# Two of the delta rule's gate projections moved forward in a hybrid decoder layer's list of dense work

## The chip, the cores and the metric

The kernel is one program on one NeuronCore of a Trainium2 chip. The metric is the device time of one execution in microseconds; smaller is better. Five engines run their own instruction queues in order and meet through semaphores: TensorE (PE, matmuls and transposes), VectorE (DVE), ScalarE (ACT), GpSimd (POOL) and SyncE (SP, which here issues all the DMAs).

## The reference, cut to what matters

One layer of a hybrid decoder, for a prompt of 1024 tokens and 8 sequences of 4 sampled tokens (1056 columns in all, model width 1024). A normalised input goes through one input projection. Its columns feed three token mixers: a gated delta rule (4 heads of 128), an mLSTM (4 heads of 64) and a Mamba-2 SSD (4 heads of 64). Their outputs go through one output projection, and a ConvFFN follows.

```python
conv_out = silu(causal_dwconv(proj[..., :CONV_DIM]))       # q, k, v of the delta rule; x, B, C of the SSD
o_gdn, gdn_new = gdn_chunked(q, k, v, g, beta, state)
o_gdn = rms_norm(o_gdn, gdn_norm) * silu(gg)               # gg: the delta rule's gate, 4 heads x 128
h_ml = rms_norm(sigmoid(mo) * mlstm_chunked(...))          # mo: 2 tiles of 128
y_ssd = rms_norm((ssd_chunked(...) + D * x) * silu(sz))    # sz: 2 tiles of 128
mix = concatenate([o_gdn, h_ml, y_ssd])
out = mix @ w_out
```

The three recurrences run in chunks of tokens, each chunk after the one before it.

## The kernel before

Activations lie transposed: features on the 128 partitions, tokens along the row. A dense tile is one block of 128 output features for all 1056 tokens: three groups of 352 columns, each a sum over 8 blocks of the input, each product made of three fp32r matmuls (high part by high part, high by low, low by high). So a tile is 72 matmuls of 128x352 (`dense`, whose matmuls all carry line 208). The result of a group lies in one of two PSUM banks named `acc` and is scaled into SBUF by DVE (line 308).

Dense work before the output projection is in units and gates. A unit is three tiles: units 0 to 3 are the heads of the delta rule (k, q, v), 4 and 5 the SSD's groups (B, C, x), 6 and 7 the mLSTM's pairs of heads. The tiles of units 0 to 5 go through a causal convolution of width 4 and a silu, on DVE (lines 473 and 482) and ACT. A gate is one tile: `gg` 0 to 3 for the delta rule's heads, `mo` 0 and 1 for the mLSTM, `sz` 0 and 1 for the SSD. A `gg` gate takes per group a scaling, a tanh on ACT, and on DVE a product (line 431) and a product with the head's output (433); for columns whose head has not been put out yet a single product (429), with the second one done where the head's output comes (1043).

The order on PE is written out by hand and in full. A class `Weave` runs generators, each with a rank, and keeps a clock of its own (`now`), which every matmul moves on by its length. A generator yields how long the other engines are expected to need (`WAIT`) before its next step. At each turn the lowest rank that is ready goes next. The recurrences have ranks 0 to 2, the samples' streams 3 to 5, and the dense work has rank 9, so dense matmuls fill PE's queue between the steps of the recurrences, and only what is left of them can. The order of DVE, ACT, POOL and SP follows from a scheduler that goes by the program's order and priorities.

`fill` takes the dense work from the list `FILL`, each time the first entry that may go. A unit may go while fewer than two units are in work, unit 2 (whose tiles lie in the buffer `mix`) as soon as the small rows are there. The gates `gg` 0 to 3 and `mo` 0 may go once the small rows are there, `mo` 1, `sz` 0 and `sz` 1 once six of the delta rule's eight passes are done:

```python
def can(n):
    if type(n) is int:
        return (n == U_MIX and "rows" in have) or (n != U_MIX and len(live) < 2)
    return "rows" in have and MIX[n] < 5 or done["gdn"] >= 2 * (U_MIX - U_GDN + 1)
```

The phases follow each other: the delta rule (8 passes of four chunks: `gdn_starts`, `gdn_blocks`, `gdn_pres`, `gdn_scans`), then the SSD (`ssd_scans`, `ssd_posts`), then the mLSTM (`ml_pres`, `ml_scans`, `ml_posts`; 4 passes of four chunks). When the mLSTM's last normalisation is done and the list is empty, the streams of the samples and the output projection are added (`samples`, `split_mix`, `project_first`). The projection's matmuls are 128x264, one for each quarter of the tokens; their operands are `mix`, cast on ACT (line 1582) and subtracted on DVE (1583).

The last steps of an mLSTM pass are these. `kq` is transposed (line 1120 makes `kwm` of it). Each of the four chunks has matmuls with `kwm`, `E` and the state `Cb`; DVE brings `Cb` up to date with two operations (1146) that the next chunk needs, and finishes `hml` with three (1151 to 1153) behind one on ACT. The normalisation (`gated_norm`) multiplies by the gate (1059), squares on ACT, sums (1063), scales (1064), takes a power on POOL (1065), multiplies (1066), transposes on PE and writes to `mix` on ACT.

The order of the list before: 0, 2, 1, `mo` 0, 3, 4, `sz` 0, `mo` 1, 5, `sz` 1, 6, 7, `gg` 0 to 3. What really ran on PE, by the entries' rules: 0, 1, 2, `mo` 0, 3, 4, `sz` 0, `mo` 1, `sz` 1, 5, 6, 7, `gg` 0, `gg` 1, `gg` 2, `gg` 3. By the trace `mo` 0 begins at 199.9 us, unit 3 at 225.1, unit 4 at 298.9, `sz` 0 at 362.5, unit 5 at 418.4, unit 6 at 471.3, unit 7 at 525.7, `gg` 0 at 580.3, `gg` 1 at 602.4, `gg` 2 at 620.5 and `gg` 3 at 633.2.

Of the kernel before, what the change touches and what calls it, by code (L numbers as in the profile page):

```python
# [49 lines left out]
U_MIX = 2  # L50
GATES = [("gg", h) for h in range(4)] + [("mo", 0), ("mo", 1), ("sz", 0), ("sz", 1)]

FILL = [0, 2, 1, ("mo", 0), 3, 4, ("sz", 0), ("mo", 1), 5, ("sz", 1), 6, 7, ("gg", 0), ("gg", 1), ("gg", 2), ("gg", 3)]
TILE_ORDER = [(s, i) for _, _, ts in UNITS for s, i, _ in ts] + GATES


# [141 lines left out]
def kernel(ctx: ExitStack, tc: tile.TileContext, I, O):  # L198
# [174 lines left out]
    with ExitStack() as ph:  # L373
# [169 lines left out]
        def fill():  # L543

            todo = [n for n in FILL if n not in have]
            while todo:
# [1666 lines left out]
```

## Time and profile before

| | |
|---|---|
| median of three runs | 1553.21 us (1550.89 to 1555.63) |
| the profiled execution | 1549.13 us, of it the span of the profile 1547.3 us |
| PE busy | 1456.2 us, 94% of the span |
| DVE busy | 1019.2 us, 66% |
| ACT, POOL busy | 605.3 us, 604.0 us |
| mean granted PE clock | 0.977 of 2.4 GHz |

PE is the engine to watch: the time is PE's work plus the time in which PE waits or runs at its lower clock. In the chain that ended last, PE's dense matmuls are the only large entry. The stretch that the change touches is from about 200 us to 655 us; there DVE is the second busy engine.

### The profile page before, as it was taken

How to read it: one execution, taken by the hardware profiler on the slowest of the kernel's cores; microseconds unless marked ns; L12 is line 12 of the kernel's file. 1: busy time of each engine (PE TensorE's matmuls, PEld its weight loads, DVE VectorE, ACT ScalarE, POOL GpSimd, SP SyncE). 2: the span in 40 equal slices, each digit the busy share in tenths (PEclk: the TensorE clock that was granted, in tenths of full speed). 3: DMA queues.
4: the chain of work that ended last, by engine and by line, in shares of the span. 5: the costliest groups of instructions: out<-in, count | busy, mean ns of one | idle time of the engine just before them, and what ended most of it. 6: DMA issues, size and time to landing. Idle time of an engine off the chain costs nothing. (4 is left out here: it accounts for less than half of the span.)

```text
span 1547.3 us, 27515 instructions
## 1 busy us (share of the span) xinstructions
PE 1456.2 (94%) x10756; PEld 1410.7 (91%) x10756; DVE 1019.2 (66%) x2014; ACT 605.3 (39%) x1316; POOL 604.0 (39%) x671
## 2 busy tenths in 40 slices
PE   9888999989989989899798999999999999999997
PEld 8787998879989989889698999999999999999996
DVE  6889878697375457723678777666666685234447
ACT  7644544533433233524475433333333344112222
POOL 6234433342343463367430434443443341212234
PEclk9989999999999999999899999999999999999998
DMA  6011010110121042312630211222222236312304
GB/s 224 30 50 31 23 45 26 36 32 18 43 59 60 29 119 94 100 69 97 210 136 33 90 59 71 73 83 70 83 84 70 83 103 236 120 48 98 111 26 157
DMA packets 60362, 124.92 MB, mean 81 GB/s; under 512 B 15544, under 2 KB 21560, under 8 KB 59720
## 3 DMA queue, kind: packets, MB, share of 16 engines
q1 hardware_dynamic: 60232, 123.16, 23.9%
q8 instruction: 85, 1.39, 0.4%
q14 instruction: 45, 0.37, 0.1%
HBM read 97.40 MB, written 25.21 MB: 79 GB/s over the span
## 5 line engine op out<-in xcount | busy, mean ns | idle before, releaser
L208 PE MATMUL acc<-h,wh 128*128 128x264 f32 (+1 forms) x3040 | 677.2, 313 | 17.5 <-DVE pre L308 12.3
L208 PEld LDWEIGHTS acc<-h,wh 128*128 128x128 f32 x3040 | 496.6, 191 | 24.4 <-DVE pre L308 8.7
L208 PE MATMUL acc<-h,wl 128*128 128x264 f32 (+1 forms) x1528 | 466.2, 305 | 0.3 <-POOL wl L619 0.2
L208 PEld LDWEIGHTS acc<-h,wl 128*128 128x128 f32 x1528 | 290.5, 190 | 1.5 <-POOL wl L619 1.5
L208 PE MATMUL acc<-hidl,wh 128*128 128x264 f32 x576 | 163.7, 284 | 0.5 <-DVE hidl L2033 0.5
L208 PE MATMUL acc<-hidh,wh 128*128 128x264 f32 x576 | 163.9, 285 | 0.0
L208 PE MATMUL acc<-hidh,wl 128*128 128x264 f32 x576 | 163.5, 284 | 0.0
L1874 POOL TENSOR_TENSOR wl<-ws,wh 128x512 fp32r<-128x512 f32 x60 | 89.3, 1495 | 161.0 <-ACT wh L1873 156.4
L2056 DVE TENSOR_TENSOR fa<-fa,acc 128x264 f32<-128x264 f32 x160 | 68.2, 427 | 125.6 <-PE acc L208 125.1
L272 POOL TENSOR_TENSOR wl<-w,wh 128x1024 fp32r<-128x1024 f32 x42 | 104.1, 2479 | 70.3 <-ACT wh L271 67.5
L208 PE MATMUL acc<-n,wh 128*128 128x264 f32 x640 | 119.3, 284 | 0.6 <-DVE n L1948 0.6
L208 PEld LDWEIGHTS acc<-hidl,wh 128*128 128x128 f32 x576 | 108.6, 189 | 0.7 <-DVE hidl L2033 0.7
L208 PEld LDWEIGHTS acc<-hidh,wl 128*128 128x128 f32 x576 | 108.6, 189 | 0.0
L208 PEld LDWEIGHTS acc<-hidh,wh 128*128 128x128 f32 x576 | 108.5, 188 | 0.0
L2047 POOL TENSOR_TENSOR wl<-w,wh 128x1024 fp32r<-128x1024 f32 (+1 forms) x22 | 47.6, 2163 | 147.7 <-ACT wh L2046 144.8
L208 PEld LDWEIGHTS acc<-n,wh 128*128 128x128 f32 x640 | 98.7, 188 | 0.8 <-issue 0.8
L1874 POOL TENSOR_TENSOR wl<-w,wh 128x512 fp32r<-128x512 f32 x40 | 64.9, 1625 | 81.0 <-ACT wh L1873 75.3
L208 PE MATMUL acc<-n,wl 128*128 128x264 f32 x320 | 91.4, 286 | 2.7 <-POOL wl L1874 2.7
L208 PE MATMUL acc<-r,wh 128*128 128x264 f32 x480 | 90.5, 286 | 2.8 <-DVE rs L1850 2.8
L208 PEld LDWEIGHTS acc<-r,wh 128*128 128x128 f32 x480 | 73.9, 188 | 4.6 <-DVE rs L1850 4.6
L1806 DVE SCALAR_TENSOR_TENSOR fy<-fpre,vec,fy 128x1072 f32<-128x1072 f32 x44 | 75.1, 1730 | 3.2 <-ACT fy L217 2.7
L2046 ACT CAST wh<-w 128x1024 fp32r<-128x1024 f32 (+1 forms) x22 | 20.5, 933 | 132.4 <-PE acc L208 127.8
(533 smaller groups left out, 3034.0 us busy)
## 6 DMA issues: line engine op xcount, KB each, us to landing
w<-in_w_in_dram SPq DMA_DIRECT2D x30, 512.0 KB
w<-in_w_up_dram SPq DMA_DIRECT2D x60, 256.0 KB
hid_dram<-hid SPq DMA_DIRECT2D x22, 528.0 KB
hidl<-hid_dram SPq DMA_DIRECT2D x21, 528.0 KB
w<-in_w_dn_dram SPq DMA_DIRECT2D x17, 512.0 KB
w<-in_w_out_dram SPq DMA_DIRECT2D x16, 512.0 KB
E<-rows_dram SPq DMA_DIRECT2D x24, 256.0 KB
n<-in_w_up_dram SPq DMA_DIRECT2D x20, 256.0 KB
```

The lines of the kernel that those rows point to most:

```text
L208: return nc.tensor.matmul(out, **kw)
L272: tt(out=wl[:, ks], in0=w[:, ks], in1=wh[:, ks].bitcast(F32), op=ALU.subtract)
L1806: stt(out=y[:, :LF], in0=pre[:, j:j + LF], scalar=col(V_FW + 3 * f + j), in1=y[:, :LF], op0=ALU.mult, op1=ALU.add)
L1874: tt(out=wl, in0=x, in1=wh.bitcast(F32), op=ALU.subtract)
L2046: nc.scalar.copy(out=wh, in_=w)
L2047: gtt(out=wl, in0=w, in1=wh.bitcast(F32), op=ALU.subtract)
L2056: vtt(out=fa[:, q, m, :], in0=fa[:, q, m, :], in1=ps[:, :Q], op=ALU.add)
```

## The change

One list is changed: `gg` 0 comes behind unit 2 and `gg` 1 behind `mo` 0.

```diff
-FILL = [0, 2, 1, ("mo", 0), 3, 4, ("sz", 0), ("mo", 1), 5, ("sz", 1), 6, 7, ("gg", 0), ("gg", 1), ("gg", 2), ("gg", 3)]
+FILL = [0, 2, ("gg", 0), 1, ("mo", 0), ("gg", 1), 3, 4, ("sz", 0), ("mo", 1), 5, ("sz", 1), 6, 7, ("gg", 2), ("gg", 3)]
```

What runs on PE by the entries' rules is now 0, 1, 2, `gg` 0, `mo` 0, `gg` 1, 3, 4, `sz` 0, `mo` 1, `sz` 1, `gg` 2, 5, 6, 7, `gg` 3. Up to the end of unit 2 nothing changes. `gg` 2 moves too, though its place in the list does not: when `sz` 1 is done, two units are still in work, so unit 5 may not go and `gg` 2 is the first entry that may. Three gates, 216 dense matmuls, so leave the end of the mixing phase, and one stays. The steps of the recurrences keep their own order. The number of matmuls is the same.

While the delta rule's last pair of passes is prepared, PE's order has 30, 42, 21, 84, 21 and 51 dense matmuls in a row (unit 4 and the end of unit 3), with four or eight transposes or four products between them. Before, the same preparation lay under unit 4 together with a whole pass of the scan.

PE's queue, the last chunk of the mLSTM's last pass and the end of its normalisations. `mc<-Cb` is the product with the state, `gsq` the transposes of a normalisation, `acc<-h` 128x352 a dense matmul and 128x264 one of the projection. Before:

```order
L208 MATMUL mb<-va_5824,kwm 128x130
L208 MATMUL mc<-va_5824,E_6336 128x130 x2
L208 MATMUL mc<-Cb,kq 128x130
L208 MATMUL acc<-h_155,wh 128x352
L208 MATMUL acc<-h_163,wh 128x352
L208 MATMUL acc<-h_155,wl 128x352
L208 MATMUL acc<-h_156,wh 128x352
L208 MATMUL acc<-h_164,wh 128x352
L208 MATMUL acc<-h_156,wl 128x352
L212 MATMUL mb<-con,gsq 128x128 x4
```

Now, from the third chunk to the projection's first matmuls:

```order
L212 MATMUL mb<-con,mix 128x128 x4
L208 MATMUL mb<-va_6111,kwm 128x130
L208 MATMUL mc<-va_6111,E_6623 128x130 x2
L208 MATMUL mc<-Cb,kq 128x130
L208 MATMUL mb<-va_6111,kwm 128x130
L208 MATMUL mc<-va_6111,E_6623 128x130 x2
L208 MATMUL mc<-Cb,kq 128x130
L212 MATMUL mb<-con,gsq 128x128 x4
L212 MATMUL mb<-con,mix 128x128 x4
L212 MATMUL mb<-con,gsq 128x128 x4
L208 MATMUL acc<-h_6850,wh 128x264
L208 MATMUL acc<-h_6852,wh 128x264
```

Behind the transposes of `kq` in the last pass the order before had runs of 9, 6, 9, 9, 6, 21, 42 and 114 dense matmuls (216) before the projection; now it has none.

DVE's queue from `kwm` of the last pass on. Before:

```order
L1120 TENSOR_TENSOR kwm<-mb,wk__6354 128x512
L429 SCALAR_TENSOR_TENSOR mix<-pre 128x32
L431 SCALAR_TENSOR_TENSOR pre<-pre 128x320
L433 TENSOR_TENSOR mix<-mix,pre 128x320
L1146 SCALAR_TENSOR_TENSOR Cb<-Cb,wib,mb 64x65 x2
L1151 TENSOR_TENSOR dn<-dn,em 128x2
L1152 RECIPROCAL dn<-dn 128x2
L1153 TENSOR_TENSOR hml<-mc,dn 128x128
L1059 SCALAR_TENSOR_TENSOR hml<-mb,hml 128x512
L1146 SCALAR_TENSOR_TENSOR Cb<-Cb,wib,mb 64x65 x2
```

Now:

```order
L1120 TENSOR_TENSOR kwm<-mb,wk__6641 128x512
L1583 TENSOR_TENSOR h_6871<-mix,h_6869 128x1056
L1146 SCALAR_TENSOR_TENSOR Cb<-Cb,wib,mb 64x65 x2
L429 SCALAR_TENSOR_TENSOR mix<-pre 128x32
L1151 TENSOR_TENSOR dn<-dn,em 128x2
L431 SCALAR_TENSOR_TENSOR pre<-pre 128x320
L1146 SCALAR_TENSOR_TENSOR Cb<-Cb,wib,mb 64x65 x2
L1059 SCALAR_TENSOR_TENSOR hml<-mb,hml 128x512
L1151 TENSOR_TENSOR dn<-dn,em 128x2
L1152 RECIPROCAL dn<-dn 128x2
```

A subtraction for the projection's operand (line 1583) now stands between `kwm` and the first update of `Cb`, and a second one stands further down, ahead of the third update.

ACT's queue at the same place (`dn` is the operation in each chunk that line 1151 waits for; `h_6842` is the decay of the delta rule's samples, whose input comes by a DMA into a buffer of the dense work's operands; `h_6869` is the projection's operand). Before:

```order
L217 ACTIVATE dn<-mc 128x2 x2
L271 CAST wh<-w 128x1024
L217 ACTIVATE pre<-pre 128x352
L217 ACTIVATE dn<-mc 128x2
L217 ACTIVATE gsq<-hml 128x512
L217 ACTIVATE dn<-mc 128x2
L217 ACTIVATE pre<-pre 128x352
```

Now:

```order
L217 ACTIVATE h_6842<-h_6842 128x128
L217 ACTIVATE h_6842<-h_6842,sneg 128x128
L217 ACTIVATE dn<-mc 128x2
L271 CAST wh<-w 128x1024
L1582 CAST h_6869<-mix 128x1056
L217 ACTIVATE pre<-pre 128x352
L332 ACT_TABLE_LOAD
L217 ACTIVATE dn<-mc 128x2 x2
L217 ACTIVATE gsq<-hml 128x512
```

The samples' decay, a cast for the projection and a load of an activation table have moved in between the chunks.

## Rows read from the trace of the kernel before

**Rows 1.** The profile's page, busy time of each engine over the whole span.

```profile
PE 1456.2 (94%) x10756; PEld 1410.7 (91%) x10756; DVE 1019.2 (66%) x2014; ACT 605.3 (39%) x1316; POOL 604.0 (39%) x671
```

**Rows 2.** Busy time by stretch (us: PE, weight loads, DVE, ACT, POOL; clock; DMA).

```profile
200.00:299.00 99.00, 94.11 (x668) 89.48 (x667) 77.91 (x207) 46.92 (x156) 34.50 (x60) 0.98 0.11 33
299.00:363.00 64.00, 56.17 (x354) 52.60 (x353) 56.88 (x140) 24.92 (x82) 22.25 (x35) 0.95 0.10 28
363.00:418.00 55.00, 54.28 (x389) 52.48 (x388) 25.31 (x54) 19.93 (x61) 14.51 (x21) 1.00 0.13 42
418.00:526.00 108.00, 100.53 (x662) 98.00 (x661) 64.16 (x148) 38.15 (x79) 49.20 (x58) 0.97 0.16 49
526.00:602.00 76.00, 71.01 (x472) 68.52 (x471) 41.12 (x120) 24.80 (x69) 40.90 (x50) 1.00 0.31 94
```

**Rows 3.** What PE waited for from 200 to 418 us: total, times, longest.

```profile
PE mb L212 <- DVE vn L990: 4.8, 1, 4.8
PE mb L212 <- DVE E L914: 2.9, 1, 2.9
```

**Rows 4.** The stretches table around PE's two longest waits of Rows 3.

```profile
345.00:350.00 5.00, 0.32 (x2) 0.32 (x3) 4.67 (x9) 1.84 (x4) 0.86 (x3) 0.73 0.33 107
350.00:354.00 4.00, 4.00 (x17) 4.00 (x16) 2.90 (x11) 0.87 (x2) 0.00 (x0) 0.50 0.02 4
255.00:259.00 4.00, 3.97 (x20) 3.93 (x21) 2.34 (x7) 0.46 (x2) 0.00 (x0) 0.57 0.04 4
```

**Rows 5.** The same table, a stretch of dense matmuls and nothing else on PE.

```profile
627.00:644.00 17.00, 17.00 (x109) 17.00 (x108) 10.26 (x20) 6.57 (x16) 2.84 (x2) 1.00 0.43 140
```

**Rows 6.** PE in order of time around the last pass's transposes and the projection's start.

```profile
602.09 0.60 PE L212 MATMUL mb<-con,kq 128*128 128x128 f32 x4
...
603.97 0.39 PE L208 MATMUL mb<-va,kwm 128*128 128x130 f32 x2
...
644.68 0.40 PE L208 MATMUL acc<-h,wh 128*128 128x264 f32 x2
...
652.32 0.39 PE L208 MATMUL acc<-h,wh 128*128 128x264 f32 x1 [2.42 <-DVE h L1583]
```

**Rows 7.** DVE's groups by line, 526 to 655 us: count, busy us, mean ns, idle before.

```profile
L1146 DVE SCALAR_TENSOR_TENSOR Cb<-Cb,wib,mb 64x65 f32<-64x65 f32 x32 | 9.0, 280 | 2.6 <-PE mc L208 1.9 <-PE mb L208 0.2
L429 DVE SCALAR_TENSOR_TENSOR mix<-pre 128x32 f32<-128x32 f32 x4 | 6.7, 1686 | 0.7 <-ACT pre L217 0.7
...
L1066 DVE TENSOR_TENSOR gsq<-hml,gss 128x512 f32<-128x512 f32 x4 | 4.9, 1236 | 5.3 <-POOL gss L1065 5.3
L1153 DVE TENSOR_TENSOR hml<-mc,dn 128x128 f32<-128x128 f32 x16 | 4.6, 290 | 0.6
L431 DVE SCALAR_TENSOR_TENSOR pre<-pre 128x352 f32<-128x352 f32 x8 | 4.2, 524 | 3.7 <-ACT pre L217 3.6
L1151 DVE TENSOR_TENSOR dn<-dn,em 128x2 f32<-128x2 f32 x16 | 4.1, 256 | 2.0 <-ACT dn L217 1.7
L1583 DVE TENSOR_TENSOR h<-mix,h 128x1056 fp32r<-128x1056 f32 x3 | 3.9, 1301 | 0.0
L1059 DVE SCALAR_TENSOR_TENSOR hml<-mb,hml 128x512 f32<-128x512 f32 x4 | 2.7, 686 | 1.9 <-PE mb L212 1.9
L1063 DVE TENSOR_REDUCE gss<-gsq 128x8 f32<-128x512 f32 x4 | 2.7, 686 | 1.7 <-ACT gsq L217 1.6
L1152 DVE RECIPROCAL dn<-dn 128x2 f32<-128x2 f32 x16 | 2.6, 164 | 0.4
```

**Rows 8.** POOL's and ACT's groups that the last pass waits for, same stretch.

```profile
L1065 POOL TENSOR_TENSOR gss<-gss,kons 128x8 f32<-128x8 f32 x4 | 6.6, 1642 | 15.4 <-DVE gss L1064 10.9 <-DVE dn L1152 4.5
...
L1582 ACT CAST h<-mix 128x1056 fp32r<-128x1056 f32 x4 | 4.2, 1071 | 0.0
...
L332 ACT ACT_TABLE_LOAD x1 | 1.3, 1283 | 0.0
```

**Rows 9.** What PE waited for from 418 to 640 us.

```profile
PE mb L208 <- POOL xw L1198: 3.8, 3, 3.0
```

## The prediction

> **What bounds the kernel now.** I read the page first, then the table of stretches, PE's waits, and the groups by line around the end of the mixing phase. PE is busy for 94% of the span, DVE for 66% [rows 1], and every large entry of the final chain is a PE matmul. So the time is PE's work, which the change does not alter, plus the time in which PE waits or runs at its lower clock. The question is only where such time goes away and where it arises. The reader should see two kinds of stretch. Under the delta rule DVE is nearly as busy as PE: 78 of 99 us from 200 on, 57 of 64 under unit 4, where it is the busier of the two [rows 2]. PE's two long waits there, 4.8 and 2.9 us, end on DVE [rows 3], and after each PE runs for about 4 us near half clock (0.50 and 0.57) [rows 4]. From 526 to 602 us, under the mLSTM, DVE has 41 us of work in 76, and the clock stays at 1.00 [rows 2]: there the dense matmuls between the chunks hide the recurrence.
>
> **What the change takes from the end.** Three gates leave the end, and by the program's order no dense matmul is left behind the last pass's transposes of `kq`. Before, PE reached these at 602.09 us and the projection's first matmul at 644.68 [rows 6], 42.6 us. Of these, 216 dense matmuls are moved away; at 109 matmuls in 17.00 us [rows 5] each takes 0.156 us, so 33.7 us. What remains of the old interval is 42.6 - 33.7 = 8.9 us: the small matmuls, and short waits.
>
> Now that interval is as long as the chain behind the transposes, and the chain runs almost wholly through DVE's queue. With the means of rows 7 and 8: `kwm` and the dense group's scaling ahead of it, about 1.9 us (between 602.09 and the first product with `kwm`, which came at 603.97 before [rows 6]); four chunks, each 2 x 0.28 + 0.26 + 0.16 + 0.29 = 1.27, so 5.1; two normalisations, each 0.69 + 0.69 + 0.16 + 1.24 = 2.8, so 5.6; two waits for POOL's power, 2 x 1.64 = 3.3, in which DVE's in-order queue stands still; two subtractions of 1.30 that now stand between the chunks, 2.6; what is left of `gg` 3 (lines 429, 431, 433), 1.69 + 0.5 + 0.5 = 2.7; ACT's square, the copies of the state and PE's last transposes, about 1.5. The sum is 22.7 us. Where no POOL operation falls on lines 429 and 1066 (I read their long means as such collisions, and take an undisturbed 1066 to be like 1059, of the same shape, 0.69) it is 20.1. I take 21.5. So the end costs 21.5 - 8.9 = 12.6 us. Beside it, the projection's own wait for line 1583, 2.4 us [rows 6], shrinks to about half, since the splits now lie ahead of it: -1.2.
>
> Two more terms belong to the end. First, ACT and DVE have the samples' decay ahead of some chunks' work. Its input is a DMA into a buffer that the dense operands free only in the last tile, so it can be late; nothing in the trace of before shows that wait on this path, so I bound it: 0 if the data is there, 4 us if two state transfers of 512 KB go ahead of it. I take 1, nearer to nothing, since the buffer is freed some 6 us before the end of dense work. Second, PE is idle for about 16 of the 21.5 us. Each wait of 3 to 5 us was followed by about 4 us near half clock, which is 2 us lost [rows 4]. I take 2 for the restart and 2.5 for the end's own small matmuls, which are 5 us of PE at full clock and about half on the chain: 4.5 us, between 2 and 8. The end in all: 12.6 - 1.2 + 1 + 4.5 = 16.9 us slower, between 11 and 26.
>
> One rule of the Trainium skill, SBUF — State Buffer, section "Who interferes with whom", bears on the two DVE lines with long means. It says that a DVE operation with two SBUF inputs and a GpSimd operation that reads SBUF exclude each other, whichever started first. The trace agrees: line 429 writes 32 columns and takes 1.69 us in the mean, longer than the subtraction of 1056 columns [rows 7]. By the rule the end would be 22.7 us if POOL's weight subtractions meet both lines and 20.1 if neither; the value taken lies between.
>
> **What it gives back under the delta rule.** The gates arrive where PE waited for DVE. A gate asks little of DVE: per tile three scalings and six products like those of line 431, 0.52 us each [rows 7], about 4.7 us beside 72 x 0.156 = 11.2 us of PE; under unit 4 DVE has 57 us beside 56 of PE. What there is to win from 200 to 418 us is bounded: PE's idle time there is 99 - 94.1 + 64 - 56.2 + 55 - 54.3 = 13.4 us, and the lower clock takes 2% of 99 and 5% of 64, so 5 us; 18 in all [rows 2].
>
> Of the two long waits I credit the earlier one, 2.9 us and 2 for its clock, since unit 3's convolutions no longer lie beside that chain. Small ones give another 0.8. The later one, under unit 4, I do not credit. There DVE has 57 us of work, and that work stays together: three convolution tiles and the preparation of the last two passes. What leaves this stretch is PE's work, a pass of the scan. Counting the program's order, about 249 dense matmuls (39 us) and some 5 us of others now stand beside the same DVE work, some 60 us with the end of unit 3. DVE can trail by about a tile, 10 us, because `sz` 0 and `mo` 1 ask little of it. So 60 - 44 - 10 = 6 us of waiting at least where 7.8 us were [rows 2], and up to 16: I put it at 2.7 worse. Together -3 us, between -10 and +9.
>
> **Under the SSD and the mLSTM** the steps and their dense neighbours are the same except that the first batch of the SSD begins under `gg` 2, which asks less of DVE than unit 5 does. The wait of 3.0 us for POOL there [rows 9] may shrink; I credit 1 us, between -5 and +3. The loads of weights change order on SP, but each tile's load is still a tile ahead, and PE has no wait for such a load from 200 to 640 us; that is costed at nothing.
>
> **The sum** is 16.9 - 3 - 1 = 12.9 us, on the profiled execution's 1549.1 us: 1562.0. That execution is 4.1 us under the median of the runs, so the forecast for the median is 1553.2 + 12.9 = 1566 us.
>
> **Rivals.**
>
> *The delta rule pays more than the end costs (faster).* The place is 200 to 418 us. If the gates let DVE catch up wherever it was late, all 18 us there come back, with another 5 around the SSD's start; against the end's low bound of 11 that is 12 us faster, 1541. The point from which it decides: the gain must pass the cost of the end, so at least 11 of 18 us must return. For it: both long waits end on DVE. Against it: the longer one lies where DVE's work is not thinned.
>
> The Trainium skill, Perfetto Trace Analysis, section "Optimization Strategy", states the rule behind this rival: where the most contended engine changes between regimes, interleaving the regimes may help. No run here shows yet whether that outweighs the uncovered end.
>
> *They cancel (within 0.3%).* 0.3%, or 4.7 us, is about what a measurement of this kernel can tell from no change. The end near 12 us and 8 to 15 us regained give 1549 to 1558.
>
> *The end is longer than its chain (slower still).* In the chunks ACT's operation `dn` stands behind the samples' decay, a cast of 1.07 us and a table load of 1.28 us [rows 8], and the decay stands behind a DMA. If every chunk meets a late head of a queue, the end's interval grows from 21.5 to about 30, and with it the time at the lower clock: 26 us in the end and 27 in all with no gain elsewhere, 1580.
>
> That the change does nothing is excluded: by the program's order 216 matmuls move.
>
> **How the numbers follow.** The forecast, slower by 5 to 20 us around 1566, has 0.63; the longer end, 1575 to 1590, has 0.15; cancelling has 0.14; the delta rule's win has 0.08. So faster 0.08, same 0.14, slower 0.78. The bounds of the unknown terms (end 11 to 26, delta rule -10 to +9, SSD -5 to +3) cannot all be at one side; for 8 in 10 I take -1 to +30 us: 1552 to 1583.
>
> **What would show it.** In the profile after: an interval of about 21 us, and not 9, between the last transposes of `kq` and the projection, with PE idle for some 16 of it, its waits ending on DVE's `kwm`, `Cb`, `gsq`, and a lower clock there; no wait for line 914 near the former 252 us; a wait of some 5 us still under unit 4. The forecast is wrong if the end's interval is under 15 us, if PE's idle time from 200 us to the end of `gg` 2 falls by more than 10 us, or if the gates' scaling on DVE makes PE wait for an `acc` bank.

## The result and the profile after

The changed kernel takes 1569.8 us in the median (1568.3 to 1573.8) against 1552.1 before: ratio 1.012, 95% interval 1.0097 to 1.0143. It is slower by about 18 us, where 12.9 were forecast. The profiled execution took 1568.33 us against 1549.13, 19.2 more, and its span is 19.2 us longer.

PE's work is unchanged. From the page of the changed kernel, the engines' busy time (it answers to [rows 1]):

```profile
PE 1457.7 (93%) x10756; PEld 1411.9 (90%) x10756; DVE 1019.3 (65%) x2016; ACT 607.0 (39%) x1316; POOL 601.8 (38%) x671
```

So the 19.2 us are waits and lower clock. To see where they lie, I cut both traces at the same points of PE's program (the first dense matmul of a tile) and took off the dense matmuls that a stretch gained or lost, at 0.156 us each [rows 5]:

| stretch | before, us | after, us | matmuls moved | left |
|---|---|---|---|---|
| to the end of unit 2 (nothing changed) | 199.9 | 198.6 | 0 | -1.3 |
| from there to the end of `sz` 1 | 218.6 | 240.0 | +144, 22.5 us | -1.1 |
| to the end of unit 7 | 161.9 | 181.5 | +72, 11.2 us | +8.4 |
| the last gates, to the projection | 64.4 | 46.1 | -216, 33.7 us | +15.4 |
| the projection to the end | 902.6 | 900.4 | 0 | -2.2 |

The last two rows together are the end: +13.2. The third, under the SSD, is what the forecast did not have. Cut once more at the start of unit 6, gate 2 and unit 5 cost 11.3 us (75.4 against 52.9, less the gate's 11.2), and 2.9 come back under units 6 and 7.

Two limits of this table matter below. It takes off dense matmuls only: twelve transposes, which take 1.15 us, lie behind the end of `sz` 1 now and lay ahead of it before, so the second row is nearer to 0 and the third nearer to +7.3. And kernels further down that keep one of the two orders on PE show how far a row moves by itself. The second stays within 0.2 us. The third spans 161.0 to 166.3 us for the order before and 181.5 to 184.4 for the changed one, most of it under unit 7. The fourth spans 64.4 to 67.4 for the order before. What repeats to 0.1 us is the interval from the last transposes of `kq` to the projection: 42.6 us in four profiles of the order before, 20.9 in four of the changed one.

**The end.** PE in order of time from the last transposes of `kq` to the projection; a line gives the start, the duration, the instruction and, in brackets, the idle time before it with what ended it:

```profile
645.24 0.60 PE L212 MATMUL mb<-con,kq 128*128 128x128 f32 x4
647.17 0.49 PE L208 MATMUL mb<-va,kwm 128*128 128x130 f32 x2 [1.34 <-DVE kwm L1120]
...
650.44 0.49 PE L208 MATMUL mc<-Cb,kq 128*128 128x130 f32 x2 [1.43 <-DVE Cb L1146]
...
653.37 1.21 PE L208 MATMUL mc<-va,E 128*128 128x130 f32 x4 [1.78 <-DVE hml L1153]
...
658.72 0.63 PE L212 MATMUL mb<-con,gsq 128*128 128x128 f32 x4 [1.98 <-DVE gsq L1066]
...
665.41 1.08 PE L212 MATMUL mb<-con,gsq 128*128 128x128 f32 x4 [5.63 <-DVE gsq L1066]
666.15 0.79 PE L208 MATMUL acc<-h,wh 128*128 128x264 f32 x2
```

From 645.24 to 666.15 are 20.9 us, where [rows 6] had 42.6 with 216 dense matmuls in it. Every wait ends on DVE. The stretches table of this interval and of the 4 us behind it (PE, weight loads, DVE, ACT, POOL; clock; DMA):

```profile
645.20:666.20 21.00, 8.84 (x55) 7.75 (x53) 15.46 (x42) 7.72 (x13) 5.64 (x3) 0.77 0.24 76
666.20:670.20 4.00, 4.00 (x20) 4.00 (x19) 1.84 (x2) 2.74 (x3) 0.00 (x0) 0.50 0.61 189
```

PE is idle for 12 us of 21, and starts the projection at half clock. DVE's queue in the same interval:

```profile
646.44 0.68 DVE L1120 TENSOR_TENSOR kwm<-mb,wk__6641 128x512 f32<-128x512 f32 x1
647.33 2.54 DVE L1583 TENSOR_TENSOR h<-mix,h 128x1056 fp32r<-128x1056 f32 x1 [0.21 <-ACT h L1582]
...
650.41 0.19 DVE L429 SCALAR_TENSOR_TENSOR mix<-pre 128x32 f32<-128x32 f32 x1
...
654.10 1.26 DVE L1583 TENSOR_TENSOR h<-mix,h 128x1056 fp32r<-128x1056 f32 x1
...
657.88 0.69 DVE L1066 TENSOR_TENSOR gsq<-hml,gss 128x512 f32<-128x512 f32 x1 [1.64 <-POOL gss L1065]
...
664.58 0.69 DVE L1066 TENSOR_TENSOR gsq<-hml,gss 128x512 f32<-128x512 f32 x1 [1.75 <-POOL gss L1065]
```

The two stops for POOL's power (1.64 and 1.75) and the two subtractions of line 1583 stand in the chain, as the sum had them. The first subtraction ran beside POOL's weight subtraction and took 2.54 us, the second 1.26; lines 429 and 1066, which met no POOL operation this time, took 0.19 and 0.69.

**The SSD.** PE's waits from 438 to 515 us of the changed kernel (in total, times, longest; it answers to [rows 9], where the same steps had one long wait of 3.0):

```profile
PE acc L208 <- DVE pre L308: 6.1, 2, 4.2
PE mb L208 <- POOL xw L1198: 3.3, 1, 3.3
```

Two causes, one behind each line. The first pass of the SSD waits for `xw`, which needs the decay rows that a DMA brings. SP's queue before them, in the changed kernel:

```profile
442.50 0.33 SPq L270 DMA_DIRECT2D w<-in_w_in_dram  x1
443.05 0.80 SPq L1186 DMA_DIRECT2D E<-rows_dram  x2
```

and what SP's queue waited for there:

```profile
SPq L270 <- POOL wl L272: 6.5, 1, 6.5
SPq L1186 <- PE mb L212: 0.4, 1, 0.4
```

The load of the next tile's weights stood for 6.5 us at the head of the queue for a buffer, with the decay rows behind it. The rows' own condition was met earlier than the second line says: before, where they were issued first at this place, they went at 414.91 us, 0.67 us after PE began the transposes of `on` (414.24), and 0.64 to 0.92 us after them in every run below that has no weight load ahead of them. Here these transposes began at 439.98, so the rows went 3.07 us after, some 2.4 us late.

In the second pass DVE is what stands still. DVE's queue there, with PE's row that waits for it last:

```profile
471.39 1.44 DVE L473 SCALAR_TENSOR_TENSOR kq<-pre,cw,kq 128x352 f32<-128x352 f32 x2
477.71 1.29 DVE L1211 TENSOR_TENSOR E<-mb,E 128x512 f32<-128x512 f32 x2 [4.88 <-POOL xw L1198]
478.92 0.52 DVE L482 SCALAR_TENSOR_TENSOR kq<-pre,kq 128x352 f32<-128x352 f32 x1
479.35 0.52 DVE L308 TENSOR_TENSOR pre<-acc,rs 128x352 f32<-128x352 f32 x1
```

```profile
480.01 0.93 PE L208 MATMUL acc<-h,wh 128*128 128x352 f32 x2 [4.25 <-DVE pre L308]
```

Line 1211 overwrites the decay that `xw` reads, so it waits for POOL's `xw`, and the scaling of a dense group (308) stands behind it: PE has no free `acc` bank, and the dense work that should hide the recurrence waits for the recurrence. Some 2.8 of the 4.9 us are spent before `xw` could start anywhere: ACT ends the decay that `xw` reads at 475.65 us.

### The profile page after: what moved, and what is told of

Same layout as the page of the kernel before. It is cut to its first block, busy times and chain, and to the rows that moved or that the text cites. A ratio compares the mean times of both kernels' runs of the same rounds, so it can differ in the third digit from the quotient of the medians.

```text
span 1566.5 us, 27531 instructions
## 1 busy us (share of the span) xinstructions
PE 1457.7 (93%) x10756; PEld 1411.9 (90%) x10756; DVE 1019.3 (65%) x2016; ACT 607.0 (39%) x1316; POOL 601.8 (38%) x671
## 5 line engine op out<-in xcount | busy, mean ns | idle before, releaser
L208 PE MATMUL acc<-h,wh 128*128 128x264 f32 (+1 forms) x3040 | 679.1, 314 | 24.4 <-DVE pre L308 22.5
```

Source lines behind the costliest of these rows:

```text
L208: return nc.tensor.matmul(out, **kw)
```

## The experiments

All ratios are to the kernel before, run on the same chip; 0.1% is 1.55 us. My theory after the result: two losses, the uncovered end and the SSD. The rival: early gates cost by delaying unit 3 and the delta rule, each its share.

**One early gate.**

```diff
-FILL = [0, 2, ("gg", 0), 1, ("mo", 0), ("gg", 1), 3, 4, ("sz", 0), ("mo", 1), 5, ("sz", 1), 6, 7, ("gg", 2), ("gg", 3)]
+FILL = [0, 2, ("gg", 0), 1, ("mo", 0), 3, 4, ("sz", 0), ("mo", 1), 5, ("sz", 1), 6, 7, ("gg", 1), ("gg", 2), ("gg", 3)]
```

> Only gate 0 goes early (behind unit 2); gates 1, 2 and 3 stay behind unit 7. My theory: the loss is made of two places, the uncovered end (216 dense matmuls gone from it) and the SSD's start, which lies later since gate 2 is run ahead of unit 5. Here 72 of the 216 are gone from the end, so its interval is 42.6 - 11.2 = 31.4 us, longer than the chain of 20.9 us that the changed kernel shows, so the end costs nothing; unit 5 follows the sz 1 gate directly, so the SSD costs nothing: 1552 us, between 1548 and 1556. Rival: each gate that stands ahead of unit 3 delays the delta rule and costs its share wherever it came from, a third of 18: 1558 us.

Measured: 1.0033 (1.0019 to 1.0048), +5 us, at the upper end of my range and near the rival's 1558, so the time does not decide. The places do. The rival's does not show: from the end of unit 2 to the end of `sz` 1 it is 229.4 us, and 218.6 + 11.2 = 229.8. The end up to the projection cost nothing, as forecast: from `gg` 1 to the projection 53.3 us, and 64.4 - 11.2 = 53.2. But units 5 to 7 cost 9.9 us more than before in the profiled run, without a gate ahead of unit 5: 0.9 under unit 5, 4.3 under unit 6 and 4.7 under unit 7. One of its waits, in unit 6's first tile, ends on a scaling as above:

```profile
487.96 0.92 PE L208 MATMUL acc<-h,wh 128*128 128x352 f32 x2 [3.72 <-DVE pre L308]
```

What held DVE here was not POOL's `xw`: it stood 2.52 us for ACT, whose queue was at the SSD's decay, and its next two products of the convolution took 3.36 us, in part beside POOL's weights. So my theory was right on the end and too narrow on the SSD. That it is enough for its passes to fall on other tiles is my reading, not shown. What the other waits of this kernel come from was not followed further; under unit 7 some 3 us may be the execution's own.

**Gate 2 held back.**

```diff
 def can(n):
...
+    if n[0] == "gg" and n[1] > 1 and 5 not in have:
+        return False
```

> The changed kernel, with gates 2 and 3 held back until unit 5 is done, so that gate 2 is not run ahead of unit 5 and two gates stand at the end. My theory: the SSD's loss of 9.7 us goes (and the 3.0 us that came back under units 6 and 7 with it), and the end has 144 dense matmuls, an interval of 42.6 - 22.5 = 20 us by PE's work against a chain of 21 to 25 us with the dense work's own scalings in DVE's queue, so 1 to 5 us are lost there: 1555 us, between 1551 and 1560. Rival (the early gates cost by their delay of unit 3): two thirds or all of the loss stays, 1564 to 1570 us.

Measured: 1.0050 (1.0023 to 1.0077), +8 us, at the upper end of my theory's range; the interval just reaches the rival's 1564. Under units 5 to 7 only 1.7 us of the 8.4 are left. In the trace (line numbers are 2 higher) the decay rows now go ahead of the weights:

```profile
439.20 0.80 SPq L1188 DMA_DIRECT2D E<-rows_dram  x2
442.24 0.33 SPq L270 DMA_DIRECT2D w<-in_w_in_dram  x1
```

The end costs 7.2 us by the table's cut and 6.1 by the interval (26.3 us, of it 72 dense matmuls, 11.2), more than my 1 to 5. Two things make it. Only 72 of the 144 dense matmuls lie behind the last transposes of `kq`, and they are spent by 644.3 us, 1.7 us after the last normalisation began. And that normalisation is longer than in the changed kernel, since its power (line 1067 here) stands behind a subtraction of weights on POOL:

```profile
645.29 3.00 POOL L272 TENSOR_TENSOR wl<-w,wh 128x1024 fp32r<-128x1024 f32 x1 [9.88 <-ACT wh L271]
648.25 1.91 POOL L1067 TENSOR_TENSOR gss<-gss,kons 128x8 f32<-128x8 f32 x1
```

**Both gates behind unit 3.**

```diff
-FILL = [0, 2, 1, ("mo", 0), 3, 4, ("sz", 0), ("mo", 1), 5, ("sz", 1), 6, 7, ("gg", 0), ("gg", 1), ("gg", 2), ("gg", 3)]
+FILL = [0, 2, 1, ("mo", 0), 3, ("gg", 0), ("gg", 1), 4, ("sz", 0), ("mo", 1), 5, ("sz", 1), 6, 7, ("gg", 2), ("gg", 3)]
```

> Gates 0 and 1 both go behind unit 3, ahead of unit 4, so that they do not delay unit 3 and the delta rule's last two heads; gates 2 and 3 stay at the end. My theory: as with gates 2 and 3 held back, the end has 144 dense matmuls and loses 1 to 5 us, and the delta rule gives back 0 to 3: 1553 us, between 1549 and 1559. Rival A (the place decides: beside unit 4's convolutions the gates thin DVE's work, and the wait of 4.8 us there and its lower clock go): 1546 to 1549 us. Rival B (gates ahead of the SSD's units delay them and cost by that): 1560 us or more.

Measured: 1.0031 (1.0017 to 1.0044), +5 us: my theory. The edit moves one thing more: in the trace `sz` 1 now runs behind unit 5. From the end of unit 2 to `gg` 2 the time is 0.9 us longer than before with the two gates' work added, so the place beside unit 4 gave nothing and the delay cost next to nothing. The end costs 7.3 us. Its last wait on PE, ahead of the projection:

```profile
650.61 1.09 PE L212 MATMUL mb<-con,gsq 128*128 128x128 f32 x4 [9.46 <-DVE gsq L1066]
651.35 0.79 PE L208 MATMUL acc<-h,wh 128*128 128x264 f32 x2
```

144 dense matmuls would be enough for the interval's length, but only 66 of them lie behind the last transposes of `kq`; they are spent by 641.1 us, as the last normalisation begins, and this is left bare. It is drawn out as well: one product of a gate (line 433) takes 2.55 us beside POOL's weights. By the number of gates left at the end, the interval less its dense matmuls is longer than the 8.9 us of before by nothing (four), nothing (three, 8.7 us), 6.1 and 9.4 (two), 12.0 us (one).

**An extra gate tile at the end, of the changed kernel and of the one before.** The list gets a second `("gg", 3)` at its end.

> The changed kernel with a seventeenth gate tile behind gate 3: gate 3 is computed and applied a second time, 72 more dense matmuls, 11.2 us of PE's work at full clock (the delta rule's last head comes out multiplied twice). My theory: PE is idle for 16 us at the end, waiting for DVE's chain, so the extra matmuls go into the idle time: between 0 and +4 us against the changed kernel, 1570 to 1574 us, and PE's interval from the last transposes of kq to the projection stays at 21 to 25 us. Rival (the end's chain is stretched by whatever stands beside it, or the loss is not idle time): +11 us, 1581 us.

> The kernel before with a seventeenth gate tile behind gate 3 (gate 3 computed and applied a second time), the control for the same addition to the changed kernel. My theory: before, the end has enough dense work to hide the chain, so 72 more matmuls cost their full 11.2 us: +10.5 to +12 us against before, where the changed kernel took only 6.7 us for them, of which 2.8 us by the projection's start. Rival (the addition costs the same wherever it stands): +6 to +8 us.

Measured: 1.0158 (1.0139 to 1.0178) for the changed kernel, 1.0095 (1.0073 to 1.0117) for the one before. 11.2 us of matmuls cost about 6 us more in the one (1 to 11), more than my 0 to 4, and 15 in the other (11 to 18). The interval from the last transposes of `kq` to the projection says it without the executions' own differences: with the extra tile it is 26.3 us where it was 20.9 in the changed kernel, 5.4 more, and 54.1 where it was 42.6 in the kernel before, 11.5 more. So about half of the added work went into idle time, as it should if the end lacks cover; before, all of it was paid.

**`xw` on DVE.**

```diff
-            gtt(out=xw, in0=xd, in1=bc(E[:, :, :, P - 1].rearrange("p h u -> p u h"), 3, 64), op=ALU.mult)
+            vtt(out=xw, in0=xd, in1=bc(E[:, :, :, P - 1].rearrange("p h u -> p u h"), 3, 64), op=ALU.mult)
```

> The changed kernel with xw (line 1198, one product of 128x512 per SSD pass, four in all) on DVE instead of POOL, so that neither PE's product with xw nor DVE's line 1211, which overwrites the decay that xw reads, waits behind POOL's queue. My theory: under the SSD's second pass DVE stood still for 4.9 us at the head of its queue on POOL's xw, with the scaling of a dense group behind it, and PE's dense work stood behind that; with xw on DVE, PE's wait of 4.25 us near 476 us falls under 2 us, the one of 3.28 us near 451 us falls to about 2 us, and the time falls by 3 to 7 us against the changed kernel: 1565 us, between 1562 and 1568. Rival (the SSD's loss is DVE's amount of work or the late rows, not POOL's place in the chain): the wait of 4.25 us stays or is found again one tile on, 1568 to 1572 us.

Measured: 1.0094 (1.0071 to 1.0117), 4 us less than the changed kernel by the middles, though the two intervals overlap. DVE no longer stops for POOL. It stops 2.92 us for ACT's decay instead, and PE's wait is 1.80 where it was 4.25; the lower clock behind it is gone. This run's rows of DVE and PE, and the stretches table of the 19 us from 480, first of the changed kernel (clock 0.84) and then of this one (1.00):

```profile
474.84 1.49 DVE L1198 TENSOR_TENSOR xw<-xd,E 128x512 f32<-128x512 f32 x1 [2.92 <-ACT E L217]
476.91 0.56 PE L208 MATMUL acc<-h,wh 128*128 128x352 f32 x2 [1.80 <-DVE pre L308]
```

```profile
480.00:499.00 19.00, 18.99 (x114) 19.00 (x115) 14.12 (x35) 6.74 (x13) 5.10 (x8) 0.84 0.20 60
```

```profile
480.00:499.00 19.00, 17.18 (x114) 16.63 (x113) 15.40 (x37) 7.54 (x18) 6.60 (x10) 1.00 0.20 60
```

The first pass's wait went from 3.28 only to 2.79, where I had expected about 2: what is left of it is the rows, as the next run shows.

**The decay rows from ACT's queue, and both edits.**

```diff
-                dma(out=ef, in_=rows_dram[4 + h, t0:t0 + 512].partition_broadcast(P))
+                nc.scalar.dma_start(out=ef, in_=rows_dram[4 + h, t0:t0 + 512].partition_broadcast(P))
```

> The changed kernel with the loads of the SSD's decay rows (line 1186) issued from ACT's queue instead of SP's, so that they no longer stand behind the next tile's weight load (line 270), which waited 6.5 us at the head of SP's queue. My theory: that wait made the rows of the first pass late by 2 to 4 us; issued near 440.5 us instead of 443.05, they land some 2.5 us earlier, PE's wait for xw near 451 us falls from 3.28 us to about 1 us, and with its lower clock 2 to 4 us come back: 1566 to 1568 us. Rival (the rows were not what the chain waited for, POOL's and ACT's queues were): the wait stays at about 3 us, 1569 to 1571 us; ACT's queue, which now waits for the rows' buffer, may hold a scaling's tanh and make it worse.

> The same with xw on DVE as well. If both waits are separate and each is what the theory says, the gains add: 4 us from xw and 2 to 4 from the rows, 1562 us, between 1560 and 1565, which is the uncovered end alone. Rival (one hides the other): 1565 us.

Measured: 1.0078 (1.0050 to 1.0106) with the rows alone, somewhat better than expected, 1.0061 (1.0038 to 1.0083) with both, as expected. From ACT's queue the rows went 0.64 us after PE began the transposes of `on` (438.89 and 438.25), where it was 3.07. PE's waits from 436 to 513 us, first with the rows from ACT, then with both:

```profile
PE acc L208 <- DVE pre L308: 4.6, 3, 4.0
PE mb L208 <- POOL xw L1198: 1.0, 1, 1.0
```

```profile
PE acc L208 <- DVE pre L308: 2.1, 2, 1.6
...
PE mb L208 <- DVE xw L1198: 0.4, 1, 0.4
```

Each edit takes its own wait. Of the 11.3 us under gate 2 and unit 5, 8.4 are left with `xw` on DVE, 4.2 with the rows from ACT, and 2.6 with both, of which the transposes that moved are 1.15. Over units 5 to 7 the 8.4 us become 6.2, 5.9 and 2.0; part of that difference is unit 7, which moves by 3 us between profiles of one order. By the runs, one edit alone is not clear of the changed kernel's interval (1.0097 to 1.0143); both together are. What is left of the loss is the end: 12.0 us in the interval, less 2.6 behind the projection, against +9.5 in the runs' ratio (6 to 13). The two causes under the SSD are shown.

**The same edits on the kernel before.**

> The kernel before with xw on DVE instead of POOL. The same theory: PE's wait of 3.01 us for xw near 446 us falls to about 1 us and the 3.4 us of lower clock behind it may go: 2 to 4 us faster than before, ratio 0.9975 to 0.9987. Rival (DVE is the tighter engine there, and 0.7 us more on it costs as much as the wait gives): ratio 0.999 to 1.002.

> The kernel before with the decay rows' loads issued from ACT's queue. There the first pass has no weight load ahead of its rows, the second has one. If the second pass's wait for xw (3.0 us near 446 us) comes from that, 2 to 4 us faster than before, ratio 0.9975 to 0.999; if it comes from POOL's own work between the rows and xw, no change, 0.999 to 1.001.

> The kernel before with both: rows by ACT's queue and xw on DVE. If both are worth there what they are in the changed kernel, 0.994; as the kernel before lost only 3.0 us and its lower clock at that place, 3 to 5 us at most, ratio 0.997 to 0.998; rival: no change, 0.999 to 1.001, since with one edit alone the wait of 3 us did not move.

Measured: 0.9996 (0.9981 to 1.0012) with `xw` on DVE, 0.9999 (0.9984 to 1.0014) with the rows from ACT, 0.9998 (0.9982 to 1.0014) with both. No change, the rival's value each time: the wait for `xw` stays at about 3 us in all three. Why it stays with the rows alone was not followed. With `xw` on DVE, it comes late because of what stands ahead of it in DVE's queue:

```profile
440.35 4.32 DVE L473 SCALAR_TENSOR_TENSOR kq<-pre,cw,kq 128x376 f32<-128x376 f32 x2
444.59 0.51 DVE L308 TENSOR_TENSOR pre<-acc,rs 128x352 f32<-128x352 f32 x1
445.03 0.67 DVE L1198 TENSOR_TENSOR xw<-xd,E 128x512 f32<-128x512 f32 x1
```

Two products of the convolution took 4.32 us, while POOL was at work. The edits mend what the change broke and nothing else, and no version here beats the kernel before.

## Why the prediction held, and where it did not

- **The interval at the end**: 21.5 us forecast (20.1 to 22.7), 20.9 measured, by the same chain: `kwm` after 1.93 us (1.9), the power 3.4 (3.3). The subtractions took 3.8 instead of 2.6, and lines 429 and 1066 met nothing. Against 8.9 before it costs 12.0 (12.6). The rival of a longer end, about 30 us, so did not come either.
- **What lies ahead of the interval** was not in the sum: 15.4 - 12.0 = 3.4 us. That the change costs this is not shown. Of the two waits there, the one of 2.06 us for `kwm` at 633.88 is no longer than in the kernel before with `xw` on DVE, which has the same order on PE (1.0 in the profile of the kernel before itself); only the one of 1.93 for `Cb` at 641.07 is (0.9 in both):

```profile
PE mb L208 <- DVE kwm L1120: 2.6, 1, 2.6
```

- **The wait for line 1583** was to halve (-1.2); it is gone (-2.4).
- **The samples' DMA** at the head of ACT's queue: 1 us forecast, none seen. ACT had done the decay by 643.0, ahead of the interval.
- **The lower clock** of the end: 4.5 us forecast. The restart is there, 4 us at 0.50 is 2 us; the 2.5 us for the end's own small matmuls did not come on top, as I read it because the next wait for DVE took them in: PE was to be idle for some 16 us and was for 12. In all the end was forecast at 16.9 and is 13.2, or 9.8 without the 3.4 us ahead of the interval.
- **The delta rule**: -3 us forecast (-10 to +9), -1.1 measured, and about 0 with the moved transposes counted where they lie. The wait near 252 us shrank to 1.83 instead of going, and its lower clock went. Unit 4 was forecast 2.7 worse; its waits only took other forms, 2.9 us for a scaling and 1.1 for `vn` instead of 4.8 for `vn`. PE's waits from 198 to 438 us after, beside [rows 3]:

```profile
PE acc L208 <- DVE pre L308: 4.0, 3, 2.9
...
PE mb L212 <- DVE E L914: 1.8, 1, 1.8
...
PE mb L212 <- DVE vn L990: 1.1, 1, 1.1
```

  So the opportunity was small, and the rival in which it pays for the end had no ground: the run with both gates beside unit 4 shows the same. The third sign of being wrong, a wait for an `acc` bank through the gates' scaling, did not come: these waits for line 308 lie under unit 4, whose own groups are scaled there.
- **The SSD** is the step that failed: -1 us forecast between -5 and +3, and +8.4 measured (7.3 without the transposes), outside the bounds. Two sentences were wrong. "The loads of weights change order on SP ... costed at nothing" looked only at whether a tile's own load is late, and not at what else stands behind it in SP's queue: the decay rows. And the sentence that `gg` 2 asks less of DVE than unit 5 priced the neighbour's amount of work, when what decided was which instruction stands at the head of DVE's queue while POOL's chain runs.

The direction and the size of the whole were right because the largest term, the end, was: it was read from the durations of a chain that the trace of before showed in full. From 12.9 us forecast to 19.2 in the profiled run: 9.4 more under the SSD, 1.9 more under the delta rule, 3.7 less at the end, and 1.3 less by which the two runs differ before the change begins. That the whole still fell between 5 and 20 is in part luck: without the 3.7 us that the end was priced too high, it would have been 22.9.

The rule on interleaving regimes (the Trainium skill, Perfetto Trace Analysis, section "Optimization Strategy") says it may help; here it gave next to nothing under the delta rule and took 12.0 us in the interval at the end. The rule on exclusion between DVE and GpSimd (the Trainium skill, SBUF — State Buffer, section "Who interferes with whom") agrees with the one subtraction of 2.54 us beside POOL's weights, against 1.26 alone.

## What to carry to other kernels

Dense work that nothing waits for is cover; what counts is where it is missing when it has been moved, and the bare chain that is left can be summed from durations of the trace before. Cover must also last to the final step of that chain: two gates were long enough here and still left 6 to 9 us, because half of them lay ahead of the chain, the rest was spent before its last step, and weights on POOL and the gates' own products on DVE drew that step out. When work moves, read every in-order queue it shifts, DMA issue too: ask which instruction will stand at each queue's head, how long it waits there, and who is behind it.

## What the runs showed that was not expected

A weight load that waited 6.5 us for its buffer at the head of SP's queue delayed a load for another consumer, and to issue that one from ACT's queue took PE's wait there from 3.28 to 0.99 us and, by the traces, gave back 7.1 us under gate 2 and unit 5 (2.5 with units 6 and 7 counted in; by the middles of the ratios, 1.012 and 1.0078, it was 6.5, but these intervals overlap). A recurrence and the dense work meant to hide it can stop each other through one in-order engine: POOL's `xw`, with the decay on ACT ahead of it, held DVE for 4.9 us, DVE's scaling held PE's bank, and PE lost 4.25 us and ran at a lower clock (0.84 of full over the next 19 us) with dense matmuls at hand.
